# An encoder layer on one core: other distance between operands and weights, a cut product, other slots, a later preparation

## Chip, cores and metric

The kernel runs on one core of one Trainium2 chip. The metric is the device time of one execution in microseconds (us). Before the change, three runs gave 856.64, 856.88 and 858.42 us; their median is 856.88.

## What is computed

One layer of an encoder: a half-step gated FFN, a mixing part (a Fourier mixer for half of the channels, attention for the other half), a second half-step FFN and a final norm. 512 positions, 1024 channels, FFN width 2752, everything in float32. The change lies in the two FFNs alone:

```python
def swiglu(h, w_gate, w_up, w_down):
    return (jax.nn.silu(h @ w_gate) * (h @ w_up)) @ w_down

x = x + 0.5 * swiglu(rms_norm(x, ffn1_norm), ffn1_w_gate, ffn1_w_up, ffn1_w_down)
...
x = x + 0.5 * swiglu(rms_norm(x, ffn2_norm), ffn2_w_gate, ffn2_w_up, ffn2_w_down)
return rms_norm(x, final_norm)
```

## The kernel before

**High and low parts.** Each float32 operand is split into a high part, rounded to the type fp32r (a cast on ACT), and a low part (the rest, a subtraction on DVE, helper `lows`, L118). A product is three matmuls: high x high, high x low, low x high. Each matmul of a 128x128 weight tile is a pair: a weight load (PEld in the profile) and the matmul itself.

**The stages of one FFN** (`ffn`, called twice, n_ = 0 and 2). The width of 2752 is 21 blocks of 128 and a tail "t" of 64. `groups` cuts the blocks in four groups. The first group is *plain*: gate and up products of 512 columns (`gate`), then the down products of the group. All other blocks go through a seven-product scheme (Strassen's, in the form with 15 additions; `seven`, `step`, `multiply`), which computes gate and up of one block from seven products of half the size in place of eight. Its moving operands are the tile `rt` (seven combinations of the normalized input h, high and low, 256 columns), made once per FFN by `operands`; its stationary operands are sums and differences of the gate and up weights, made per block by `prepare`.

**Order.** For each later group, first a run of five or six blocks through `seven` (one block ahead of the group: blocks 4 to 9, 10 to 15, 16 to 20 in the first FFN, 3 to 8, 9 to 14, 15 to 20 in the second), then the eight down products (`down`, output blocks d = 0 to 7, 512 columns), and behind d = 0 the last product of the run's last block (`rest`, step 9). So there are six runs. In a run, block j has the steps 0 (a11), 1 (a12), 9 of the block before (a22), 3 (s1), 4 (s2), 5 (s4), 6 (s3): each is one `multiply` of twelve pairs, four 128-row pieces by three passes, 256 columns wide, at L382. Steps 0, 4, 6 and 9 accumulate in one PSUM bank (r), steps 3 and 5 in another (q), step 1 in a third (p). `kept` (L390) copies an intermediate state of a bank to SBUF on ACT: p1 after step 0, p5 after step 3, u2 after step 4. Step 6 goes on writing bank r, so it must wait for the copy u2.

**Preparation.** While block j is multiplied, `prepare` makes the weights of block j + 1. It issues two DMAs of 512 KB on SP's queue (raw_g, raw_u) and returns eight pieces of work, which are emitted between the steps as `PIECES` says: casts of high parts on ACT (L343 for pairs such as s1 and s2, L352 for a22), their low parts on DVE (L118) and the sums and differences on DVE (L358). The pieces of the first block of a run are emitted among the down products of the group before.

**Slots.** The weights' high and low parts lie in the tile `ring`: 12 slots of 4 KB per partition. The first eight are `own`, the last four `shared`; the shared ones are also the `plain` slots that the down weights use. `take` gives out the slot that has been free longest, from the own ones first, or from the shared ones first if `most` is set; `give` returns a slot when the product that reads it has been emitted. `most` is set for the preparation of the last block but one of each run.

**Addresses.** `room` puts unused bytes ahead of a tile. The ring starts at byte 16512 of each partition, `at` (the FFN's activations) at 118656, `rt` at 147392; slots, pieces and passes lie multiples of 256 bytes apart.

**Queues.** On PE and SP the instructions stand in the order in which the kernel emits them. On ACT and DVE the framework's scheduler orders them by its own simulation of the program, so that a change of slots or emission can reorder those two queues. In the mixing part between the FFNs the order of all queues is written out by hand; the change does not reach it.

Of the kernel before, what the change touches and what calls it, by code (L numbers as in the profile page):

```python
# [29 lines left out]
HALF = S // 2  # L30
USES = "a11", "a12", "s1", "s2", "s4", "s3", "a22"
PIECES = (0, 2, 2, 1, 1, 1, 1)
KH = KD // 2
HI_DVE = ("f0", "f1")
SWAP_DMA = ("q1", "q2", "q3")

# [43 lines left out]
def encoder(ctx, tc, A, out):  # L80
    nc = tc.nc
# [5 lines left out]
    def room(pool, n):  # L87


        pool.tile([P, n // 4], F32, name=f"room{len(rooms)}")  # L90
        rooms.append(n)
# [6 lines left out]
    def bank(name):  # L98
        return pp.tile([P, S], F32, tag="bank", name=name)
# [150 lines left out]
    def ffn(norm, after, wgu, wd, wdt, groups, opening, closing):  # L250
# [6 lines left out]
        with tc.tile_pool(name=f"act{n_}", bufs=1) as ap, tc.tile_pool(name=f"sums{n_}", bufs=2) as sp:  # L257
            room(ap, 192)
            at = ap.tile([P, PLACES, 2, S], F32R, name=f"at{n_}")
            room(ap, 64)  # L260
            rt = ap.tile([P, 7, 2, KH, HALF], F32R, name=f"rt{n_}")
            wt = []
            free, where = list(range(PLACES)), {}
# [5 lines left out]
            own, shared = slots[:KD], slots[KD:]  # L269
# [26 lines left out]
            def operands(rp, i0, i1):  # L296
                for i in range(i0, i1):
                    b = sp.tile([P, 4, HALF], F32, tag="raw_g", name=f"b{n_}_{i}")
                    for o, k in ((0, i), (2, i + KH)):
                        nc.vector.scalar_tensor_tensor(  # L300
# [15 lines left out]
            def back(ts):  # L316
                plain[:] = [t for t in plain if all(t is not q for q in ts)]

            def take(most):

                pool = (shared or own) if most else (own or shared)
                taken.append(pool.pop(0))
                return taken[-1]

# [2 lines left out]
                    taken[:] = [q for q in taken if q is not t]  # L327
                    (shared if any(t is q for q in slots[KD:]) else own).append(t)

            def prepare(j, most=False):  # L330

                g = sp.tile([P, KD * P], F32, tag="raw_g", name=f"raw_g{n_}_{j}")
                u = wp.tile([P, KD * P], F32, tag="raw", name=f"raw_u{n_}_{j}")
                for t, c in ((g, 2 * j), (u, 2 * j + 1)):
                    nc.sync.dma_start(out=t.rearrange("p (a b) -> p a b", b=P), in_=wgu[c])
                a11, a12, a21, a22 = g[:, :S], g[:, S:], u[:, :S], u[:, S:]
                s12 = sp.tile([P, 2 * S], F32, tag="s12", bufs=1, name=f"s12_{n_}_{j}")
                s34 = sp.tile([P, 2 * S], F32, tag="s34", bufs=1, name=f"s34_{n_}_{j}")
                w = {}

                def both(names, src):
                    hi, lo = (take(most and names[0] != "a11") for _ in range(2))
                    nc.scalar.copy(hi, src)  # L343
                    lows(lo, src, hi)
                    for i, n in enumerate(names):
                        w[n] = tuple(t[:, i * S : (i + 1) * S] for t in (hi, lo))
                    w[max(names, key=USES.index), "slots"] = hi, lo

                def single(n, src):
                    t = take(False)  # L350
                    hi, lo = t[:, :S], t[:, S:]
                    nc.scalar.copy(hi, src)  # L352
                    lows(lo, src, hi)
                    w[n] = hi, lo
                    w[n, "slots"] = (t,)

                def combine(out, a, b, op):
                    nc.vector.tensor_tensor(out=out, in0=a, in1=b, op=op)  # L358

                return w, [  # L360
                    (both, ("a11", "a12"), g),
                    (combine, s12[:, :S], a21, a22, ALU.add),
                    (combine, s12[:, S:], s12[:, :S], a11, ALU.subtract),
                    (both, ("s1", "s2"), s12),
                    (single, "a22", a22),
                    (combine, s34[:, :S], a11, a21, ALU.subtract),
                    (combine, s34[:, S:], a12, s12[:, S:], ALU.subtract),
                    (both, ("s3", "s4"), s34),
                ]

            def seven(js, done):

                done = [done]
                banks = {}

                def multiply(ps, wn, on, w, first):

                    (whi, wlo), (mhi, mlo) = w[wn], (part[on][:, i] for i in range(2))
                    for i in range(KH):
                        ks = slice(i * P, (i + 1) * P)  # L380
                        for o, (a, b) in enumerate(((whi, mhi), (whi, mlo), (wlo, mhi))):
                            nc.tensor.matmul(  # L382
                                ps, a[:, ks], b[:, i], start=first and i == 0 and o == 0,
                                stop=i == KH - 1 and o == 2, skip_group_check=not first,
                            )
                    give(*w.get((wn, "slots"), ()))

                def kept(ps, n, j):
                    t = sp.tile([P, HALF], F32, tag=n, name=f"{n}{n_}_{j}")
                    nc.scalar.copy(t, ps)  # L390
                    return t

                def step(j, w, n):
                    b = banks.setdefault(j, {})
                    if n == 0:
                        b["r"] = bank(f"r{n_}_{j}")[:, :HALF]
                        multiply(b["r"], "a11", "b11", w, True)
                        b["p1"] = kept(b["r"], "p1", j)
                    elif n == 1:
                        ps = bank(f"p2{n_}_{j}")[:, :HALF]  # L400
                        multiply(ps, "a12", "b21", w, True)
                        b["g"] = tp.tile([P, S], F32, tag="g", name=f"g{n_}_{j}")
                        nc.vector.tensor_tensor(out=b["g"][:, HALF:], in0=ps, in1=b["p1"], op=ALU.add)
                    elif n == 3:
                        b["q"] = bank(f"q{n_}_{j}")[:, :HALF]
                        multiply(b["q"], "s1", "t1", w, True)
                        b["p5"] = kept(b["q"], "p5", j)
                    elif n == 4:
                        multiply(b["r"], "s2", "t2", w, False)
                        b["u2"] = kept(b["r"], "u2", j)  # L410
                    elif n == 5:
                        multiply(b["q"], "s4", "b22", w, False)
                        nc.vector.tensor_tensor(out=b["g"][:, :HALF], in0=b["q"], in1=b["u2"], op=ALU.add)
                        nc.scalar.activation(b["g"], b["g"], AF.Silu)
                    elif n == 6:
                        multiply(b["r"], "s3", "t3", w, False)
                        b["u"] = tp.tile([P, S], F32, tag="u", name=f"u{n_}_{j}")
                        nc.scalar.copy(b["u"][:, :HALF], b["r"])
                        nc.vector.tensor_tensor(
                            out=b["u"][:, :HALF], in0=b["u"][:, :HALF], in1=b["p5"], op=ALU.add  # L420
                        )
                    elif n == 9:
                        multiply(b["r"], "a22", "t4", w, False)
                        u, i = b["u"], place(j)
                        h, l = at[:, i, 0], at[:, i, 1]
                        nc.scalar.copy(u[:, HALF:], b["r"])  # L426
                        nc.vector.tensor_tensor(out=u, in0=b["g"], in1=u, op=ALU.mult)  # L427
                        nc.scalar.copy(h, u)
                        lows(l, u, h)
                        del banks[j]  # L430

                for s in range(7 * len(js)):
                    i, n = divmod(s, 7)
                    if n == 2 and i:
                        step(js[i - 1], done[i - 1][0], 9)
                    if n == 0 and i + 1 < len(js):
                        done.append(prepare(js[i + 1], i + 1 == len(js) - 2))
                        ahead = list(done[-1][1])
                    if n != 2:
                        step(js[i], done[i][0], n)  # L440
                    if i + 1 < len(js):
                        for _ in range(PIECES[n]):
                            f, *a = ahead.pop(0)
                            f(*a)
                return lambda: step(js[-1], done[-1][0], 9)
# [27 lines left out]
            for gi, group in enumerate(groups):  # L473
                last = gi == len(groups) - 1
# [3 lines left out]
                else:  # L478
# [8 lines left out]
                    for i, c in enumerate(left):  # L487
                        pss.setdefault(c // 2, []).append(gate(c, by_dma=i in (1,) if n_ else i > 0))
                        if due:
                            j = due.pop(0)  # L490
# [3 lines left out]
                        while len(parts) * len(left) > (len(left) - 1 - i) * KH:  # L494
                            o = parts.pop(0)
# [14 lines left out]
                for d in range(KD):  # L510
# [5 lines left out]
                    ps = bank(f"dn{n_}_{d}_{gi}")  # L516
# [3 lines left out]
                    for _ in range(len(group) - (last and d < 2)):  # L520
                        next(steps)
                    waiting.append((d, ps, steps))
                    if d == 1 and not last:
                        ready = prepare(groups[gi + 1][0] + 1)
                        ahead.extend(ready[1])
                    if d == 0:
# [904 lines left out]
```

## Time and profile before

| | |
|---|---|
| median of three runs | 856.88 us |
| span of the profiled execution | 855.1 us |
| matmuls, and weight loads | 5434 each |
| matmuls at L382 | 2940 (1680 into r, 840 into q, 420 into p) |
| bytes moved by DMA | 89.25 MB, on average 104 GB/s |

The profiled execution's own device time is not listed beside its span; the median of the runs is 1.8 us above the span. The page gives busy time for each engine, the chain of work that ended last, and groups of like instructions: line, engine, operation, output<-inputs, shapes, count | busy us, mean ns of one | idle time before. Matmuls are pipelined and their ends are modelled, so a matmul's duration is longer than the period at which they follow each other. Stretches (from:to in us) give width, busy time and, in brackets, the instructions in them; where no engine is chosen, in the order PE, PEld, DVE, ACT, POOL; then granted clock, share of DMA and GB/s. Rows of the chain in order of time give start, length, engine, tile, line and count.

### The profile page before, as it was taken

What the parts mean: (1) busy time and instruction counts of PE and PEld (TensorE: products, weight loads), DVE (VectorE), ACT (ScalarE), POOL (GpSimd) and SP (SyncE); (2) the same over time, 40 slices, a digit from 0 to 9 for tenths busy, and PEclk for the clock granted to TensorE, in tenths of its full rate; (3) what the DMA queues carried; (4) which work ended last, traced back from release to release, by engine and by line L of the source; (5) the groups of instructions that cost most, each with busy time, mean ns of one, the idle gap of its engine ahead of it and who ended that gap; (6) DMA issues with size and microseconds to landing.
All of it is one profiled execution on the core that took longest, in us unless ns stands there. A gap on an engine that the chain in (4) does not pass through costs nothing.

```text
span 855.1 us, 13706 instructions
## 1 busy us (share of the span) xinstructions
PE 846.4 (99%) x5434; PEld 765.5 (90%) x5434; DVE 641.5 (75%) x1007; ACT 467.9 (55%) x781; POOL 33.3 (4%) x35
## 2 busy tenths in 40 slices
PE   9999999999999999999999999999999999999996
PEld 7878998899989998889988888899989998899986
DVE  7998985488756937699999478999846985488453
ACT  7763764266524635677776347656632764266352
POOL 0110000000000000222000000100000000000001
PEclk9999999999999999999999999999999999999998
DMA  6664322323243113414020224553232331323213
GB/s 250 164 157 157 118 88 74 118 99 127 74 145 109 48 56 111 148 50 136 26 74 26 99 70 116 120 196 108 77 117 100 118 106 56 117 100 113 67 43 99
DMA packets 31424, 89.25 MB, mean 104 GB/s; under 512 B 3712, under 2 KB 9344, under 8 KB 31232
## 3 DMA queue, kind: packets, MB, share of 16 engines
q1 hardware_dynamic: 28320, 82.87, 28.6%
q0 software_dynamic: 2496, 4.99, 3.2%
q8 instruction: 42, 0.69, 0.3%
q10 hardware_dynamic: 544, 0.52, 0.2%
q14 instruction: 22, 0.18, 0.1%
HBM read 83.91 MB, written 2.10 MB: 101 GB/s over the span
## 4 chain that ended last, share of the span: by engine, by line
PE 97%; DVE 1%; DMA 0%; issue 0%; ACT 0%; POOL 0%; POOLq 0%; DVEq 0%; ACTq 0%
PE r L382 23%; PE q L382 12%; PE dn L157 8%; PE dn L155 8%; PE dn L156 8%; PE p L382 6%; PE mix L155 3%; PE mix L157 3%; PE mix L156 3%; PE gu L632 3%; PE gu L155 2%; PE gu L157 2%; PE gu L156 2%; PE mix L1122 2%; PE mix L1079 2%; PE mix L928 1%
## 5 line engine op out<-in xcount | busy, mean ns | idle before, releaser
L382 PE MATMUL r<-rt,ring 128*128 128x256 f32 x1680 | 216.8, 280 | 0.0
L382 PEld LDWEIGHTS r<-rt,ring 128*128 128x128 f32 x1680 | 205.6, 188 | 2.6
L157 PE MATMUL dn<-at,ring 128*128 128x512 f32 x300 | 117.0, 390 | 0.5 <-DVE ring L118 0.5
L155 PE MATMUL dn<-at,ring 128*128 128x512 f32 x300 | 117.0, 390 | 0.0
L156 PE MATMUL dn<-at,ring 128*128 128x512 f32 x300 | 116.7, 389 | 0.0
L382 PE MATMUL q<-rt,ring 128*128 128x256 f32 x840 | 109.8, 279 | 0.0
L382 PEld LDWEIGHTS q<-rt,ring 128*128 128x128 f32 x840 | 103.5, 188 | 0.0
L468 DVE SCALAR_TENSOR_TENSOR gx<-dn,gx 128x512 f32<-128x512 f32 x61 | 42.0, 688 | 75.2 <-PE dn L157 75.2
L118 DVE TENSOR_TENSOR ring<-s,ring 128x1024 fp32r<-128x1024 f32 x70 | 85.3, 1220 | 16.5 <-PE r L382 10.5
L147 ACT CAST ring<-raw_dn 128x768 fp32r<-128x768 f32 (+3 forms) x58 | 45.5, 787 | 87.0 <-PE dn L156 70.6
L343 ACT CAST ring<-s 128x1024 fp32r<-128x1024 f32 x70 | 73.5, 1050 | 34.8 <-PE r L382 17.9
L157 PEld LDWEIGHTS dn<-at,ring 128*128 128x128 f32 x300 | 56.3, 188 | 13.0 <-DVE ring L118 1.1
L156 PEld LDWEIGHTS dn<-at,ring 128*128 128x128 f32 x300 | 56.3, 188 | 11.3
L155 PEld LDWEIGHTS dn<-at,ring 128*128 128x128 f32 x300 | 56.3, 188 | 11.3
L118 DVE TENSOR_TENSOR ring<-raw_dn,ring 128x768 fp32r<-128x768 f32 (+3 forms) x58 | 51.6, 892 | 6.1 <-ACT ring L147 4.1
L382 PE MATMUL p<-rt,ring 128*128 128x256 f32 x420 | 54.9, 279 | 0.0
L118 DVE TENSOR_TENSOR ring<-raw_g,ring 128x1024 fp32r<-128x1024 f32 x35 | 42.8, 1223 | 14.7 <-PE p L382 8.4
L382 PEld LDWEIGHTS p<-rt,ring 128*128 128x128 f32 x420 | 51.7, 188 | 0.0
L343 ACT CAST ring<-raw_g 128x1024 fp32r<-128x1024 f32 x35 | 36.8, 1051 | 21.5 <-DMA raw_g<-in_wgu 8.8
L352 ACT CAST ring<-raw_u 128x512 fp32r<-128x512 f32 x35 | 21.8, 622 | 33.5 <-PE dn L157 15.1
L427 DVE TENSOR_TENSOR u<-g,u 128x512 f32<-128x512 f32 x35 | 24.0, 686 | 16.0 <-ACT u L426 16.0
L224 POOL TENSOR_TENSOR r<-ms,mhalf 128x4 f32<-128x4 f32 (+1 forms) x5 | 5.9, 1179 | 679.9 <-DVE ms L217 679.9
(309 smaller groups left out, 1584.4 us busy)
## 6 DMA issues: line engine op xcount, KB each, us to landing
raw_g<-in_wgu SPq DMA_DIRECT2D x35, 512.0 KB, 3.7
raw_u<-in_wgu SPq DMA_DIRECT2D x35, 512.0 KB, 4.3
raw_dn<-in_wd SPq DMA_DIRECT2D x40, 384.0 KB, 3.1
raw_gu<-in_wgu SPq DMA_DIRECT2D x12, 512.0 KB, 3.6
raw_o<-in_wo SPq DMA_DIRECT2D x8, 512.0 KB, 3.5
raw_dn<-in_wd SPq DMA_DIRECT2D x8, 448.0 KB, 3.3
raw_wq<-in_wins SPq DMA_DIRECT2D x4, 512.0 KB, 4.6
raw_f<-in_winf SPq DMA_DIRECT2D x4, 512.0 KB, 3.5
```

The source lines that it names most:

```text
L118: nc.vector.tensor_tensor(out=lo, in0=src, in1=asf(hi), op=ALU.subtract)
L147: nc.scalar.copy(hi[:, :n, :], raw[:, :n, :])
L155: nc.tensor.matmul(ps, whi, mhi, start=first, stop=False)
L156: nc.tensor.matmul(ps, whi, mlo, start=False, stop=False)
L157: nc.tensor.matmul(ps, wlo, mhi, start=False, stop=last)
L343: nc.scalar.copy(hi, src)
L352: nc.scalar.copy(hi, src)
L382: nc.tensor.matmul(ps, a[:, ks], b[:, i], start=first and i == 0 and o == 0, stop=i == KH - 1 and o == 2, skip_group_check=not first,)
L427: nc.vector.tensor_tensor(out=u, in0=b["g"], in1=u, op=ALU.mult)
L468: nc.vector.scalar_tensor_tensor(out=x[d][:, t], in0=ps[:, t], scalar=0.5, in1=x[d][:, t], op0=ALU.mult, op1=ALU.add)
L632: nc.tensor.matmul(pss[c], w[:, k % 2, c], m[k], start=k == 0 and m is hh and w is hi, stop=k == KD - 1 and w is lo,)
L1079: nc.tensor.transpose(pts[n][:, c * P : (c + 1) * P], prob[t, b, c][:, kc * P : (kc + 1) * P], ident)
```

## The change

It has four parts, in `ffn` alone.

- `room(ap, 64)` ahead of `rt` becomes `room(ap, 192)`. In the built program `rt` then starts at byte 147520 in place of 147392, and so do the tiles behind it, 128 bytes later each.
- `multiply` gets the argument `entry`, set for step 0 of the first block of a run. There the second of the twelve products (first piece, high x low) is cut in two matmuls, of columns 0 to 63 and 64 to 255.
- `take` loses its argument: the own slots are always taken first, for every block.
- In the first group of each FFN, the preparation of the first block of the first run is emitted at d = 2 in place of d = 1.

```diff
             room(ap, 192)
             at = ap.tile([P, PLACES, 2, S], F32R, name=f"at{n_}")
-            room(ap, 64)
+            room(ap, 192)
             rt = ap.tile([P, 7, 2, KH, HALF], F32R, name=f"rt{n_}")
...
-            def take(most):
+            def take():
 
-                pool = (shared or own) if most else (own or shared)
+                pool = own or shared
                 taken.append(pool.pop(0))
                 return taken[-1]
...
-                    hi, lo = (take(most and names[0] != "a11") for _ in range(2))
+                    hi, lo = (take() for _ in range(2))
...
+                def cols(i, o, entry):
+
+                    cuts = (0, HEAD, HALF) if entry and (i, o) == (0, 1) else (0, HALF)
+                    return [slice(*c) for c in zip(cuts, cuts[1:])]
+
-                def multiply(ps, wn, on, w, first):
+                def multiply(ps, wn, on, w, first, entry=False):
...
-                            nc.tensor.matmul(
-                                ps, a[:, ks], b[:, i], start=first and i == 0 and o == 0,
-                                stop=i == KH - 1 and o == 2, skip_group_check=not first,
-                            )
+                            for c in cols(i, o, entry):
+                                nc.tensor.matmul(
+                                    ps[:, c], a[:, ks], b[:, i, c], start=first and i == 0 and o == 0,
+                                    stop=i == KH - 1 and o == 2, skip_group_check=not first or entry,
+                                )
...
-                        multiply(b["r"], "a11", "b11", w, True)
+                        multiply(b["r"], "a11", "b11", w, True, j == js[0])
...
-                        done.append(prepare(js[i + 1], i + 1 == len(js) - 2))
+                        done.append(prepare(js[i + 1]))
...
-                    if d == 1 and not last:
+                    if d == (1 if gi else 2) and not last:
                         ready = prepare(groups[gi + 1][0] + 1)
```

`HEAD` is 64.

More of the change, by code (lines that the diff above doesn't have):

```diff
@@ L33 @@
 KH = KD // 2
+HEAD = 64
 HI_DVE = ("f0", "f1")
@@ L328, in give, with prepare @@
                     (shared if any(t is q for q in slots[KD:]) else own).append(t)
-            def prepare(j, most=False):
+            def prepare(j):
                 g = sp.tile([P, KD * P], F32, tag="raw_g", name=f"raw_g{n_}_{j}")
@@ L349, in single @@
                 def single(n, src):
-                    t = take(False)
+                    t = take()
                     hi, lo = t[:, :S], t[:, S:]
```

## The prediction

> **What bounds the kernel now.** I read the page first: busy time, granted clock, the chain that ended last, the costliest groups.
>
> ```profile
> span 855.1 us, 13706 instructions
> ...
> PE 846.4 (99%) x5434; PEld 765.5 (90%) x5434; DVE 641.5 (75%) x1007; ACT 467.9 (55%) x781; POOL 33.3 (4%) x35
> ...
> PE 97%; DVE 1%; DMA 0%; issue 0%; ACT 0%; POOL 0%; POOLq 0%; DVEq 0%; ACTq 0%
> ...
> L382 PE MATMUL r<-rt,ring 128*128 128x256 f32 x1680 | 216.8, 280 | 0.0
> L382 PEld LDWEIGHTS r<-rt,ring 128*128 128x128 f32 x1680 | 205.6, 188 | 2.6
> ```
>
> TensorE is the bound: 97% of the chain, with each matmul paired with a weight load of its own (5434 of each). So the time can only move through the period at which pairs start, through the number of pairs, and through waits. The mean of 280 ns is no period, since matmuls overlap; periods come from counts in stretches. The change is aimed at the pairs of line 382. They stand in six runs, so I cut the trace into those:
>
> ```profile
> 76.36:134.79 58.43, 58.43 (x492) 1.00 0.29 100
> 168.92:227.30 58.38, 58.38 (x492) 1.00 0.29 100
> 261.44:309.93 48.49, 48.49 (x408) 1.00 0.28 91
> 562.00:619.00 57.00, 57.00 (x492) 1.00 0.31 107
> 653.11:711.50 58.39, 58.39 (x492) 1.00 0.29 100
> 745.63:804.02 58.39, 58.39 (x492) 1.00 0.27 94
> sum 339.08, PE 339.08; mean PE 56.51
> ```
>
> The first number after the count is the granted clock, 1.00. The runs hold 5 x 492 + 408 = 2868 pairs in 339.08 us. One run of 492 is 1.4 us shorter than its equals, with the same program and addresses. The chain in order of time says why:
>
> ```profile
> 562.16 1.42 PE r L382 x12
> ...
> 579.31 2.91 PE r L382 x24
> 589.03 2.93 PE r L382 x24
> 598.75 2.72 PE r L382 x24
> ...
> 772.94 2.97 PE r L382 x24
> 782.98 2.83 PE r L382 x24
> ```
>
> A pair has two steady periods: 2.83 / 24 = 117.9 ns, where every run begins (562.16: 1.42 for 12) and nearly all stay, and 2.72 / 24 = 113.3 ns, which the fourth run falls into after the wait near 579 and keeps to its end, through another wait near 589. A third period belongs to the pairs of 256 columns at the end that read "at" (the timeline, and a stretch with their count):
>
> ```profile
> 829.31 0.28 PE L155 MATMUL last<-at,ring 128*128 128x256 f32 x1
> ```
> ```profile
> 829.00:837.00 8.00, 7.69 (x65) 7.88 (x66) 0.85 (x2) 1.00 0.01 2
> ```
>
> From 829.31 to 837.00 65 begin: 7.69 / 64 = 120 ns. In the built program the weights' ring starts 128 bytes past a multiple of 256, "at" too, and rt 192 past one. So 0 bytes off goes with 120 ns, 64 bytes off with 117.9 or 113.3, and the mode, once entered, persists.
>
> The slow stretches with a wait (2.97) cost 0.14 us over those without, the fast one (2.93 against 2.72) 0.21. The timeline of one wait:
>
> ```profile
> 92.11 1.57 PE L382 MATMUL q<-rt,ring 128*128 128x256 f32 x12
> ...
> 92.19 1.05 ACT L343 CAST ring<-s 128x1024 fp32r<-128x1024 f32 x1
> ...
> 93.14 0.36 ACT L390 COPY u<-r 128x256 f32<-128x256 f32 x1
> 93.56 0.89 PEld L382 LDWEIGHTS r<-rt,ring 128*128 128x128 f32 x7
> ```
>
> The cast into a slot that step 4 has just freed stands ahead of the copy of u2 in ACT's queue; the twelve matmuls of step 5 take 1.41 us, cast and copy end at 93.50, and step 6, which writes the bank that the copy reads, waits. There are 18 such waits, three in each run: in those blocks s3's high part is given a slot freed at step 4.
>
> **The change part by part.** *rt moves by 128 bytes*, so that it lies 192 bytes off the weights, modulo 256. No matmul in the trace reads at that distance. Its period is bounded by the nearest rows: 113.3 from below, 120 from above; over 2868 pairs 325.0 to 344.2 us.
>
> *The second product of each run is cut in 64 and 192 columns*: one pair more in each of six runs. No such pair is in the trace. Its bounds are 0 (if 64 columns hide in the neighbouring loads) and the mean load of 188 ns; I take a whole fast period, because a pair comes no closer than that in these stretches: 6 x 0.113 = 0.7 us (0 to 1.1). More important is what it does to the mode. All six runs now enter at 117.9, each behind the same 512-column products, so entry is repeatable; the only change of mode came behind an irregular gap between loads (the stretch at 579.31). The cut puts one short matmul under a full weight load, so it makes just such a gap at the entry. Whether 64 columns at 192 bytes lead to 113.3 the trace cannot say. I take 113.3: it is the state that survived a wait, while in the slow one 17 of 18 waits left things as they were and one led out; in the whole trace no wait leads from fast to slow. 2868 x 0.11333 = 325.0 us.
>
> The Trainium skill, "TensorE: Matmul & The Clock Gate", Part 2 (step by step), speaks against this: TensorE has two independent SBUF read ports, and loading the next weights takes no read bandwidth from the running matmul. By that rule 128 bytes of address change nothing, and this part is worth 0 in place of the gain above. Two periods at one address do not refute it, but the rows at 0 and 64 bytes, 120 against 113.3 to 117.9 ns, do not fit it.
>
> *Plain slots taken last.* Before, the preparation of a run's last block but one took plain slots first; following the first-in-first-out lists by hand, s3's high part then waits on step 4 in three blocks of a run. After, it takes slots freed at step 4 in every prepared block: 5 + 5 + 4 + 5 + 5 + 5 = 29 waits, and in the built program's ACT queue the cast stands ahead of the copy of u2 in all of them (before, in the first three, with another cast of the same length in one case). At 113.3 ns a wait costs 0.21: 29 x 0.21 = 6.1 us. Bounds: 18 x 0.14 = 2.5, if ACT gets by as now, and 0.3 each, 8.7, if two pieces queue up.
>
> The first down weights come free a block earlier in return, and with them one low part of 0.89 us on DVE moves into blocks that also prepare. DVE is what hides the preparations:
>
> ```profile
> 579.46:598.59 19.13, 19.13 (x168) 19.00 (x168) 18.16 (x27) 13.27 (x23) 0.00 (x0) 1.00 0.34 115
> ```
> ```profile
> L118 DVE TENSOR_TENSOR ring<-raw_dn,ring 128x768 fp32r<-128x768 f32 (+3 forms) x58 | 51.6, 892 | 6.1 <-ACT ring L147 4.1
> ```
>
> Two fast blocks hold 18.16 us of DVE work, 9.1 a block. A fast block with one wait lasts 84 x 0.1133 + 0.21 = 9.7. Another 0.89 makes 10.0, so up to 0.3 a run could come out as a wait for a low part: 0 to 1.8 us; I take 0.7.
>
> *First preparation a block later.* It applies to the first group of each FFN only. SP now issues raw_dn 2 ahead of the two raw tiles of 512 KB, and ACT's cast and DVE's low part of dn 2 move ahead of the preparation's. Now that low part is late:
>
> ```profile
> 60.62 0.39 PE L155 MATMUL dn<-at,ring 128*128 128x512 f32 x1
> 60.85 0.39 PE L156 MATMUL dn<-at,ring 128*128 128x512 f32 x1
> 61.12 0.55 DVE L118 TENSOR_TENSOR ring<-raw_dn,ring 128x384 fp32r<-128x384 f32 x1
> ...
> 61.72 0.50 PE L157 MATMUL dn<-at,ring 128*128 128x512 f32 x1 [0.48 <-DVE ring L118]
> ...
> 67.13 1.22 DVE L118 TENSOR_TENSOR ring<-s,ring 128x1024 fp32r<-128x1024 f32 x1
> ```
>
> A product starts 0.23 us after the one before (60.62 to 60.85), but 0.87 passes between 60.85 and 61.72: 0.64 us that should go. Bounds 0 and 0.8 (with the refill behind it). The preparation ends later by one output block, 11 x 0.23 = 2.5 us; its last low part now ends at 68.35, and the run that reads it begins at 76.36, so 8.0 us of down products cover it; without that cover it would cost those 2.5. Nothing else is queued behind these DMAs before dn 3.
>
> **Sum.** The six runs: 325.0 + 6.1 + 0.7 + 0.7 = 332.5 against 339.1, so -6.6; the first preparation -0.6; together -7.2. The profiled span was 855.1; the runs' median is 856.88, 1.8 more, which I keep as what lies around the span. 855.1 - 7.2 + 1.8 = 849.7 us. Its own range is 846 (waits stay at 18) to 853 (DVE and ACT at their upper bounds).
>
> **The rivals.** *The slow mode stays* (the address and the cut are inert): 2868 x 0.1179 = 338.1, 29 waits at 0.14 = 4.1, cut 0.7: 342.9, +3.8; -0.6: 860.1 us. For it: every run enters slow, and the added waits are certain by the queue. Against it: the fourth run shows that the other period can be had. It decides as soon as fewer than some 30% of the pairs run at 113.3, since each tenth of them is worth 1.3 us. This is the inert outcome that the Trainium skill's rule names; the change then does not do what its first two parts could.
>
> *192 bytes off is a bad distance, as 0 is*: 2868 x 0.120 = 344.2; step 5 then lasts 1.44 us, so a wait shrinks to about 0.12, 29 x 0.12 = 3.5; cut 0.7: 348.4, +9.3, -0.6: 865.6 us. For it: 120 is the one other period seen; against it: 0 and 192 are different distances, and 64 already avoided it.
>
> *Half*: the cut leads into the fast mode, but with five waits a run it is lost again about midway: mean of the forecast and the slow case, 854.9. For it: modes change at waits. Against it: the wait at 589 did not change it.
>
> *Fast, without added waits*: 325.0 + 18 x 0.21 + 0.7 = 329.5, -9.6, -0.6: 846.7; with no wait at all 842.9. Against it: the queue's order.
>
> **How the numbers follow.** Forecast 0.46, slow mode stays 0.22, half 0.13, bad distance 0.13, fast without added waits 0.06. A change of 0.2% is 1.7 us, about what a measurement tells from none. Faster: 0.46 + 0.06 + 0.10 of half = 0.62; same: 0.03 of half and 0.05 of slow (860.1 is +0.4%, less one or two waits) = 0.08; slower: 0.17 + 0.13 = 0.30. The range runs from 844 to 861: it leaves out the bad distance and the extreme of no waits.
>
> **What would show it.** Chain pieces of twelve pairs at 1.36 from the first or second step of each of the six runs show the mode; 1.41 or 1.42 there shows the slow rival, 1.44 the bad distance. Five stretches of 24 a run near 2.93, with ACT's copy of u2 as releaser, show the waits; three would show my slot count wrong. The product at 61.72 without idle time shows the first preparation. A 64-column matmul followed by a gap over 0.19 us would make the cut dearer. The prediction falls if fewer than half the pairs run at 113.3, or if DVE's low parts end more waits than ACT.

## The result, and the profile after

The changed kernel takes 866.07 us (median of four runs, 864.66 to 866.57). The kernel before took 856.82 beside it (856.64 to 858.42). The ratio is 1.0096, with a 95% interval of 1.0079 to 1.0112: slower by 1%, where 849.7 us, 0.8% faster, had been forecast. The profiled execution took 866.55 us, of which the span is 864.7.

The page of the changed kernel: span, busy time, the chain by engine, and four groups, three of which now have idle time ahead of them (the last two columns: idle us, and what ended most of it).

```profile
span 864.7 us, 13711 instructions
...
PE 846.8 (98%) x5440; PEld 760.3 (88%) x5440; DVE 643.1 (74%) x1007; ACT 468.9 (54%) x781; POOL 32.4 (4%) x35
...
PE 92%; ACT 4%; DVE 1%; issue 1%; DMA 1%; POOL 0%; POOLq 0%; DVEq 0%; ACTq 0%
...
L389 PE MATMUL r<-rt,ring 128*128 128x256 f32 x1686 | 215.4, 280 | 4.5 <-ACT u L397 4.2
...
L156 PE MATMUL dn<-at,ring 128*128 128x512 f32 x300 | 117.2, 391 | 3.3 <-ACT ring L148 3.3
L158 PE MATMUL dn<-at,ring 128*128 128x512 f32 x300 | 117.4, 391 | 1.9 <-DVE ring L119 1.9
L157 PE MATMUL dn<-at,ring 128*128 128x512 f32 x300 | 116.8, 389 | 0.0
```

The first and the third pass of the down products (L155 and L157 there) in the page of the kernel before:

```profile
L157 PE MATMUL dn<-at,ring 128*128 128x512 f32 x300 | 117.0, 390 | 0.5 <-DVE ring L118 0.5
L155 PE MATMUL dn<-at,ring 128*128 128x512 f32 x300 | 117.0, 390 | 0.0
```

TensorE had 97% of the chain before and has 92% now. Six matmuls more are the six cuts. The rest of the loss is waiting: ahead of step 6 (bank r, for ACT's copy of u2), and ahead of the first and third pass of a down product. Where they stand, in the stretches of the six runs (width, TensorE's busy time, its matmuls, then the granted clock):

```profile
76.30:135.39 59.09, 57.80 (x494) 1.00 0.30 99
170.45:229.33 58.88, 58.05 (x494) 1.00 0.29 98
265.07:313.83 48.76, 48.18 (x410) 1.00 0.28 88
565.83:623.45 57.62, 57.62 (x494) 1.00 0.33 110
659.18:717.75 58.57, 57.65 (x495) 1.00 0.30 98
753.45:811.87 58.42, 57.54 (x495) 1.00 0.26 86
sum 341.34, PE 336.83; mean PE 56.14
```

The runs grew by 341.34 - 339.08 = 2.3 us, and everything outside them by the other 7.3 of the 9.6. Neither number shows what happened inside. For that I counted all pairs of the scheme (the six runs, and the last product of each behind the first down product) by the distance from one start to the next, without those at a wait or a cut. Before, 345 had up to 115 ns and 2559 more; now 2034 have up to 115 and 830 more. That is worth (2559 - 830) x 4.6 ns = 8.0 us, a gain. But there are 33 waits in place of 18, and the time that the pairs at them take beyond 113.3 ns each is 12.1 us in place of 3.0. With 0.8 for the cuts the three make +1.9; 2.3 were measured.

One wait, in the timeline of ACT's and TensorE's instructions (start, length, operation; idle time before and its releaser in brackets):

```profile
111.14 0.84 ACT L148 CAST ring<-raw_dn 128x768 fp32r<-128x768 f32 x1 [0.33 <-PE r L389]
...
111.88 0.62 ACT L435 CAST at<-u 128x512 fp32r<-128x512 f32 x1
112.40 1.04 ACT L344 CAST ring<-s 128x1024 fp32r<-128x1024 f32 x1
...
113.35 0.36 ACT L397 COPY u<-r 128x256 f32<-128x256 f32 x1
...
113.76 0.62 PE L389 MATMUL r<-rt,ring 128*128 128x256 f32 x3 [0.54 <-ACT u L397]
```

Three casts, 2.5 us together, stand ahead of a copy that has to be done within the 1.36 us of step 5. The forecast saw the third of them. The first is that of the first down weights. By the lists of slots, the plain slot that it fills held the low part of s1 and s2, which step 4 reads last: the cast may start when the copy may, and stands ahead of it. (The kernel before casts these weights at 124.98.) The brackets say 0.54, but the start before 113.76 lies 0.82 us back: matmuls have modelled ends, so the idle column shows a wait only where it outlasts the matmul's drawn end.

Not every wait is like this one. Of the 33, six have the cast of a down weight ahead of the copy, each time into a plain slot that the low part of s1 and s2 held until step 4: 0.8 to 1.0 us each, 5.3 in all. In five, 0.3 to 0.6 us each and 2.2 in all, no down weight is there, but the cast of `at` comes so late that it pushes the cast of s3 and s4 back. The other 22 take 4.6 us, 0.21 on average, as forecast. One of the five, in the same view of ACT:

```profile
185.69 0.62 ACT L435 CAST at<-u 128x512 fp32r<-128x512 f32 x1 [0.71 <-DVE u L434]
186.22 1.05 ACT L344 CAST ring<-s 128x1024 fp32r<-128x1024 f32 x1
187.17 0.36 ACT L397 COPY u<-r 128x256 f32<-128x256 f32 x1
```

Between the runs, in the same timeline of the changed kernel (ACT, DVE, then TensorE):

```profile
234.95 0.83 ACT L148 CAST ring<-raw_dn 128x768 fp32r<-128x768 f32 x1 [0.64 <-PE r L389]
...
235.81 0.96 DVE L119 TENSOR_TENSOR ring<-raw_dn,ring 128x768 fp32r<-128x768 f32 x1 [0.52 <-ACT ring L148]
...
235.83 0.50 PE L156 MATMUL dn<-at,ring 128*128 128x512 f32 x1 [0.80 <-ACT ring L148]
236.17 0.40 PE L157 MATMUL dn<-at,ring 128*128 128x512 f32 x1
236.83 0.50 PE L158 MATMUL dn<-at,ring 128*128 128x512 f32 x1 [0.26 <-DVE ring L119]
237.17 0.39 PE L156 MATMUL dn<-at,ring 128*128 128x512 f32 x1
```

The cast of the second down weights waited for "PE r L389": the last pairs of step 9 of the run's last block, which stand behind the first down product. By the lists that block now holds two of the four plain slots (the low part of s1 and s2, until step 4, and a22, until step 9). So the second down product waits for the cast, its third pass for the low part, and each wait has a longer gap behind it (0.34 in place of 0.23). There are four such places, and a fifth behind the first run, where only the third pass waits: there the high part goes into the slot free since step 4, the low part into that of a22. By starts, a place costs 1.0 to 1.9 us; together they cost 7.6 us, 0.3 more than the 7.3 outside the runs, where the idle time at 61.72 is gone and other small differences stand against that.

### The profile page after: what moved, and what is told of

Read it like the earlier page. It is cut to its first block, busy times and chain, and to the rows that moved or that the text cites. A ratio compares the mean times of both kernels' runs of the same rounds, so it can differ in the third digit from the quotient of the medians.

```text
span 864.7 us, 13711 instructions
## 1 busy us (share of the span) xinstructions
PE 846.8 (98%) x5440; PEld 760.3 (88%) x5440; DVE 643.1 (74%) x1007; ACT 468.9 (54%) x781; POOL 32.4 (4%) x35
## 4 chain that ended last, share of the span: by engine, by line
PE 92%; ACT 4%; DVE 1%; issue 1%; DMA 1%; POOL 0%; POOLq 0%; DVEq 0%; ACTq 0%
PE r L389 20%; PE q L389 9%; PE dn L158 8%; PE dn L157 8%; PE dn L156 8%; PE p L389 5%; PE mix L156 3%; PE mix L158 3%; PE mix L157 3%; PE gu L639 3%; PE gu L156 3%; PE gu L158 3%; PE gu L157 3%; ACT ring L344 2%; PE mix L1129 2%; PE mix L1086 2%
## 5 line engine op out<-in xcount | busy, mean ns | idle before, releaser
L389 PE MATMUL r<-rt,ring 128*128 128x256 f32 x1686 | 215.4, 280 | 4.5 <-ACT u L397 4.2
L389 PEld LDWEIGHTS r<-rt,ring 128*128 128x128 f32 x1686 | 202.8, 188 | 10.5 <-ACT u L397 7.2
L157 PE MATMUL dn<-at,ring 128*128 128x512 f32 x300 | 116.8, 389 | 0.0
L389 PE MATMUL q<-rt,ring 128*128 128x256 f32 x840 | 107.4, 277 | 0.0
L389 PEld LDWEIGHTS q<-rt,ring 128*128 128x128 f32 x840 | 101.2, 188 | 0.0
L157 PEld LDWEIGHTS dn<-at,ring 128*128 128x128 f32 x300 | 56.3, 188 | 11.3
L389 PE MATMUL p<-rt,ring 128*128 128x256 f32 x420 | 53.7, 277 | 0.0
L389 PEld LDWEIGHTS p<-rt,ring 128*128 128x128 f32 x420 | 50.6, 188 | 0.0
L435 ACT CAST at<-u 128x512 fp32r<-128x512 f32 x35 | 21.7, 621 | 14.9 <-DVE u L434 14.9
```

What stands on the lines that cost most here:

```text
L157: nc.tensor.matmul(ps, whi, mlo, start=False, stop=False)
L389: nc.tensor.matmul(ps[:, c], a[:, ks], b[:, i, c], start=first and i == 0 and o == 0, stop=i == KH - 1 and o == 2, skip_group_check=not fi ...
```

## The experiments

The column "six runs" is the sum of the kernel's stretches as above. The last column counts all pairs of the scheme, as above, by their distance from start to start. (467 of the 471 of off0 stand at 115 ns itself, among others of 117 to 122.)

| kernel | median us | before, same chip | ratio, 95% interval | six runs us | pairs up to / over 115 ns |
|---|---|---|---|---|---|
| slots_back | 849.53 | 856.17 | 0.9918 (0.9888 to 0.9948) | 334.52 | 1934 / 963 |
| slots_only | 871.15 | 856.17 | 1.0174 (1.0147 to 1.0202) | 344.62 | 575 / 2295 |
| offset_only | 851.17 | 856.17 | 0.9939 (0.9919 to 0.9960) | 332.69 | 2120 / 784 |
| cut_only | 856.57 | 856.17 | 1.0007 (0.9990 to 1.0025) | 339.83 | 435 / 2463 |
| u2_first | 842.98 | 856.63 | 0.9847 (0.9831 to 0.9862) | 326.87 | 2664 / 268 |
| after_u2 | 854.68 | 856.63 | 0.9975 (0.9966 to 0.9985) | 330.52 | 2642 / 278 |
| off0 | 861.32 | 856.63 | 1.0059 (1.0046 to 1.0072) | 343.30 | 471 / 2433 |
| off128 | 864.53 | 856.63 | 1.0096 (1.0081 to 1.0110) | 346.23 | 15 / 2889 |
| u2_all | 842.82 | 857.82 | 0.9826 (0.9812 to 0.9839) | 325.87 | 2844 / 90 |
| u2_no_cut | 854.46 | 857.82 | 0.9960 (0.9948 to 0.9973) | 337.81 | 0 / 2940 |
| u2_off64 | 855.35 | 857.82 | 0.9969 (0.9958 to 0.9981) | 338.42 | 7 / 2927 |
| u2_early | 844.12 | 857.82 | 0.9839 (0.9825 to 0.9852) | 325.86 | 2844 / 90 |

### One part undone, and three parts alone

slots_back is the changed kernel with the slots of before; the other three are parts put into the kernel before.

```diff
# slots_back, against the changed kernel
-            def take():
+            def take(most):
-                pool = own or shared
+                pool = (shared or own) if most else (own or shared)
...
-                        done.append(prepare(js[i + 1]))
+                        done.append(prepare(js[i + 1], i + 1 == len(js) - 2))
# slots_only, against the kernel before: these lines the other way round
# offset_only, against the kernel before
-            room(ap, 64)
+            room(ap, 192)
             rt = ap.tile([P, 7, 2, KH, HALF], F32R, name=f"rt{n_}")
# cut_only, against the kernel before
-                        multiply(b["r"], "a11", "b11", w, True)
+                        multiply(b["r"], "a11", "b11", w, True, j == js[0])
```

> The changed kernel with the old rule for the slots (shared ones first for a run's last block but one); address, cut and later preparation stay. Theory S (the slots cost the time: the last block of a run holds two plain slots, so the second down weights wait for one, and high casts that wait on step 4 hold up ACT): no wait over 0.3 us at the head of the down products, 18 waits of 0.2 in the runs, pairs mostly at 113.3 ns: 845 to 850 us, faster than before. Rival P (pairs at 113.3 outrun ACT and DVE, whatever the slots): waits of 0.5 to 0.9 us in the runs and at the down products stay, 858 to 866 us.

> The kernel before with the new rule for the slots alone. Theory S: waits of 1.0 to 1.9 us at the head of four or five groups of down products (some 7 us) and five longer waits a run, with pairs near 117.9 ns: 866 to 877 us, slower than the changed kernel or equal to it. Rival P: pairs stay slow enough for ACT and DVE, so at most the 11 added waits of 0.14 us: 857 to 860 us.

> The kernel before with rt 192 bytes off the weights, nothing else. If the address decides the period (A): every run enters at 113.3 ns, 846 to 849 us. If the cut is what leads into 113.3 (C): runs enter at 117.9, change only at waits, 851 to 857 us.

> The kernel before with the second product of each run cut in 64 and 192 columns, rt at 64 bytes as before. If the cut alone leads into 113.3 (C): runs enter at 113.3, 846 to 850 us. If it needs the address (A, or both together): runs enter at 117.9, 857 to 858.5 us.

The old slots take the changed kernel from 866.07 to 849.53; the new slots alone take the kernel before from 856.17 to 871.15. So this one part costs 15 to 17 us, and the other three gain 0.8%. The waits view of slots_only (engine and tile, what it waited for: us, times, longest) has the same three rows as the changed kernel, at the addresses of before:

```profile
PE r L382 <- ACT u L390: 3.4, 6, 0.6
PE dn L155 <- ACT ring L147: 3.3, 4, 0.9
PE dn L157 <- DVE ring L118: 2.4, 6, 0.7
```

In slots_back the two rows of dn are gone. Its 18 waits in the runs did not come out at 0.2 each, as expected: they take 4.7 us, the longest over 0.6, again behind a late cast of `at`. So waits of that kind come with the old slots too. The distance alone gains 0.6%, though all six runs of offset_only enter at 118 ns: each leaves that period behind one of its waits. The cut alone, at 64 bytes, leads no run into 113 ns and changes nothing that can be told.

### The copy ahead of the cast

The three casts say that the wait is a matter of ACT's order. One edge puts the cast of s3 and s4 behind the copy of u2, once with the old slots and once with the new ones.

```diff
# u2_first against slots_back, and after_u2 against the changed kernel
-                    nc.scalar.copy(t, ps)
+                    copies[n] = nc.scalar.copy(t, ps).ins
...
                             f, *a = ahead.pop(0)
-                            f(*a)
+                            with tc.issue_after(copies["u2"]) if n == 6 else nullcontext():
+                                f(*a)
```

> slots_back with one more edge: on ACT's queue the cast of s3 and s4 is issued behind the copy of u2. Slots are those of before, nothing else changes. In slots_back 18 waits of 0.15 to 0.68 us in front of step 6 add up to 4.7 us, and 963 of 2897 pairs ran at 117.9 ns, 4.4 us over 113.3. Theory Q (the waits are the copy of u2 standing behind a cast of 1.05 us in ACT's queue, and the slow period returns only through a wait): both go, 849.5 - 4.7 - 4.4 + 0.3 for the six pieces behind the down products = 840.7 us; a wait is left in block 18 at most. Half theory (waits go, period still changes on its own): 844.8. Rival R (the cast is late next, or its low part on DVE, and the product of s4 or s3 of the next block waits for it): the waits move, 848 to 851.

> The changed kernel with that same edge on ACT's queue and its own slots. It splits the cost of the slots rule in its two suspected places. In the changed kernel the waits for the copy of u2 add up to 12.1 us in 31 places, and the waits at the second and third down product behind four runs and the first to 7.7. Theory Q: the first kind goes but for the last blocks of runs, where a cast of s1 and s2 still stands ahead, about 2.5 us; the second kind stays whole: 866.1 - 12.1 + 2.5 = 856.5 us, 854 to 859, and the down products still wait 1.0 to 1.6 us each group. Rival (both kinds have one cause, slots that come free too late, and the queue's order only shows it): the time stays above 862.

u2_first took 842.98 us, between theory Q (840.7) and its half (844.8). The trace decides for Q: with the waits the second period went as well. The sum of Q had taken the waits of an execution of 851.45 us off the median of 849.53; taken off 851.45 it gives 842.7. The single wait that was left, in block 18, did lead 181 pairs back to 118 ns. after_u2 took 854.68. Its waits view:

```profile
PE dn L158 <- ACT ring L150: 3.3, 4, 0.9
PE r L391 <- ACT u L399: 2.3, 4, 0.6
PE dn L160 <- DVE ring L121: 1.9, 5, 0.7
```

The two rows of the down products are to the digit those of the changed kernel (3.3 and 1.9): that part of the cost is one of slots, not of queue order. In the runs five waits are left, 3.8 us in all, of 33 with 12.1; 2.5 had been expected. So the difference between the changed kernel and slots_back (16.5 us on medians, 15.0 between the profiled spans) has two causes, 12.1 - 4.7 = 7.4 us of waits in the runs and 7.6 at the down products. Ahead of step 6 it is the order of ACT's queue, which the new slots made worse; at the down products it is a slot held until step 9.

### The distance

In the kernel before `room(ap, 64)` ahead of `rt` becomes 128 (off0) or 256 (off128). The two names, and the expectations that go with them, have the distances the wrong way round. `rt` started at byte 147392, the ring at 16512. With 64 bytes more `rt` starts at 147456, 130944 = 511 x 256 + 128 bytes behind the ring; with 192 more it starts at 147584, 131072 = 512 x 256 bytes behind it. So off0 lies 128 bytes off the weights, modulo 256, and off128 lies 0 bytes off.

> The kernel before with rt 0 bytes off the weights modulo 256, nothing else. Theory A (the distance modulo 256 sets the period; at 0 it is the 120 ns of the pairs that read at): all pairs near 120 ns, 2868 x 0.120 = 344.2 against 339.1, less 18 waits that shrink by 0.02 each: 861 us, ratio 1.006. Rival (the address is inert, the period is chance of the entry): 856, pairs at 117.9 or 113.3.

> The kernel before with rt 128 bytes off the weights modulo 256. Theory A with a period that falls with the distance: pairs at 113.3 for more than half of the runs, 850 to 853 us, as with 192. Theory A with the banks in pairs of 128 (128 stands as 0 does): 120 ns, 861. Rival (the address is inert): 856, mostly 117.9.

Read by what was built, 0 bytes (off128) came out at 864.53 us and 128 bytes (off0) at 861.32. For 0 bytes 861 had been expected; that the kernel named off0 took just that is chance. The period is the one that theory A gave for 0 bytes, 120 ns. Its sum was short because it set 344.2, which holds no waits, against 339.1, which does: with 18 waits of 0.12 it comes to 346.4, and 346.23 were measured. For 128 bytes the form of theory A that sets 128 beside 0 gave 861, and came out. The inert address, 856, is refuted by both. The chain in order of time (start, length, pieces of 12 or 24 pairs), off128 (0 bytes) and then off0 (128 bytes):

```profile
79.98 1.44 PE q L382 x12
81.42 1.44 PE r L382 x12
...
84.30 3.03 PE r L382 x24
```
```profile
80.96 1.44 PE r L382 x12
...
86.84 1.42 PE p L382 x12
```

At 0 bytes 12 pairs take 1.44 us, 120 ns a pair, almost throughout, and none of the 18 waits changes it. At 128 bytes all six runs enter at 120 ns, and behind the first wait most pieces last 1.42 or 1.43 (118.9 ns on average over all pairs without a wait). The stretches grew from 339.1 to 346.2 us at 0 bytes and to 343.3 at 128. Only `rt` and the tiles behind it moved, and the ring did not: whether the distance counts or `rt`'s own address modulo 256, no run shows.

### No wait left

u2_all puts the edge on every cast of a preparation; the other three take one thing out of it.

```diff
# u2_all, against u2_first
-                            with tc.issue_after(copies["u2"]) if n == 6 else nullcontext():
+                            with tc.issue_after(copies["u2"]) if copies.get("u2") else nullcontext():
# u2_no_cut, against u2_all
-                    cuts = (0, HEAD, HALF) if entry and (i, o) == (0, 1) else (0, HALF)
+                    cuts = (0, HALF)
# u2_off64, against u2_all
-            room(ap, 192)
+            room(ap, 64)
             rt = ap.tile([P, 7, 2, KH, HALF], F32R, name=f"rt{n_}")
# u2_early, against u2_all
-                    if d == (1 if gi else 2) and not last:
+                    if d == 1 and not last:
```

> u2_first with the edge on all casts of a preparation, so that the last cast ahead of a copy of u2 (raw_g of block 20, in block 18) goes behind it too. u2_first had one wait left, 0.21 us and its refill, and behind it 181 pairs at 117.9 ns. Theory M (the period changes at waits alone, and the cut sets it at the entry): no wait is left, no pair changes: 843.0 - 181 x 0.0046 - 0.2 = 841.9 us. Rival: 843 or more, since the casts behind the copy come too late for block 20.

> u2_all without the cut of the second product. Theory M: without the cut all six runs enter at 117.9 ns, as in offset_only, and with no wait left nothing leads out: 841.9 + 2868 x 0.0046 - 6 x 0.1 = 854.4 us, almost all pairs at 117.9. Rival (192 bytes lead to 113.3 by themselves, after some pairs): 841 to 844.

> u2_all with rt at its old distance of 64 bytes, with the cut. Theory M with what cut_only showed (at 64 bytes the cut does not lead to 113.3): pairs at 117.9 throughout, 855 us. Rival (the cut is enough once no wait disturbs): 842.

> u2_all with the first preparation at d = 1, as before the change. If the later preparation is worth what the prediction gave it, the product at 62 us waits again for its low part, 0.6 to 0.8 us, and the time is 842.5 to 842.8 us, 0.6 to 0.9 above u2_all, in the trace more surely than in the medians. Rival (the later preparation only moves the wait): same time.

u2_all beats both kernels: 842.82 us, ratio 0.9826 to the kernel before. (841.9 had been expected. On medians it does not stand apart from u2_first, 842.98 on another chip; the spans are 840.8 and 842.4. The trace shows what theory M says: no wait in the runs, and no pair that changes.) Its stretches, first and last with the sum, and its chain:

```profile
75.51:131.41 55.90, 55.90 (x495) 1.00 0.31 105
...
733.72:789.62 55.90, 55.90 (x494) 1.00 0.31 98
sum 325.87, PE 325.87; mean PE 54.31
```
```profile
85.33 1.36 PE p L391 x12
86.69 1.36 PE r L391 x12
...
92.13 2.72 PE r L391 x24
```

All five long runs last 55.9 us, and step 5 with step 6 takes 2.72 where the changed kernel had 2.93 to 3.03. Of its 90 pairs over 115 ns 18 stand at the six entries; the other 72 are the last products behind the first down products, which begin without a cut and run at 118. Without the cut, or at 64 bytes with it, nothing is left of that. The chain of u2_no_cut:

```profile
81.32 1.41 PE q L391 x12
82.73 2.83 PE r L391 x24
85.56 1.41 PE p L391 x12
```

All 2940 pairs of it run at 118 ns, from the first to the last, and u2_off64 does the same. Against u2_all they take 11.6 and 12.5 us more. So distance and cut are worth some 12 us together, and neither alone brings a run to 113 ns, once no wait disturbs (no run leaves out both): the cut leads into 113 ns only at 192 bytes, and at 192 bytes a run that enters at 118 keeps it. That offset_only gained all the same was the work of its waits.

In u2_early the wait at the down product of 62 us is back, here in its timeline of TensorE:

```profile
61.29 0.39 PE L159 MATMUL dn<-at,ring 128*128 128x512 f32 x1
62.43 0.50 PE L160 MATMUL dn<-at,ring 128*128 128x512 f32 x1 [0.75 <-DVE ring L121]
62.77 0.40 PE L468 MATMUL dn<-at,wt 128*128 128x512 f32 x1
```

From start to start 1.14 and 0.34 us in place of 0.23 twice: 1.0 us, above the 0.6 to 0.8 expected. The medians stand 1.3 apart (842.82 and 844.12), the spans 1.4.

## Why the prediction was wrong

**The bound and the period at the entry: right, in part by luck.** TensorE's pair period decides. The changed kernel enters all six runs at 113.3 ns, as taken, and u2_no_cut shows that the cut is what leads there. But the forecast said itself that its trace could not decide between the periods; what about the cut does it, no run shows. That the state persists was right only between waits. It was argued from one run that kept it through one wait; of the 18 waits only that one fell in the fast state, so the slow state had 17, of which 16 changed nothing. In the changed kernel eleven of the 33 waits change the period, seven to 118 ns and four back to 113, and 762 pairs of the six runs had over 115: 3.5 us that the sum did not hold. It is the mechanism of the rival "half", in a smaller size.

**The step that failed: plain slots taken last.** The sum gave it "29 x 0.21 = 6.1 us", with 8.7 as the upper bound, and 0.7 for DVE. The count was nearly right (33; the four more stand in last blocks of runs), the price was not. 0.21 came from a wait with one cast ahead of the copy, and 22 waits cost that. The same paragraph said that the first down weights come free a block earlier, and followed only their low part, on DVE. That holds in the first run (cast at 111.14 in place of 124.98), but not in all: in the second their cast comes in the last block, at 225.18, where the kernel before has it at 211.84, a block ahead of the last. The step missed the cast itself. It takes 0.84 us on ACT and goes ahead of the same copy, since its slot now comes free behind step 4; five times with the first down weights and once with the second this makes waits of 0.8 to 1.0 us, 4.0 us over their price. Five waits behind a late cast of `at` are 1.2 over theirs, and the four more make 0.8. The sum is 12.1 us, 6.0 over the term, where 8.7 was the bound. u2_first and after_u2 show that the queue's order is the cause: with the copy ahead of the cast of s3 and s4 one of the 18 waits of slots_back is left, and five of the 33 of the changed kernel.

**What the step left out: who gives plain slots back.** Plain slots that the last block but one does not take are taken by the last block, which keeps one until step 9, behind the first down product. The prediction followed the first down weights alone; the second ones come late. This is the 7.6 us at the down products, which stay in after_u2 and go with the old slots. Together: 6.0 + 7.6 + 3.5 - 0.7 (no low part ended a wait inside the runs) = 16.4 us over the forecast; 866.07 - 849.7 = 16.4 were measured, so closely by chance, since terms of some 0.1 are left out.

**The cut: right.** A run of 493 pairs takes 55.90 in u2_all, and 492 x 2.72 / 24 = 55.76: 0.14 a run, 0.8 in six, where 0.7 was given.

**First preparation: right.** -0.6 was given, with 0.8 as the bound. By starts the place cost 0.75 us in the kernel before (0.87 and 0.34 in place of 0.23 twice) and costs 1.0 in u2_early. The later preparation made no run wait.

**The rule of the Trainium skill.** By the Trainium skill, "TensorE: Matmul & The Clock Gate", Part 2 (step by step), loading weights takes no bandwidth from the running matmul; from this the prediction worked out that the address would be inert. off0 and off128 move `rt` alone, with the tiles behind it, and cost 0.6% and 1.0%: for the time of these pairs the rule does not hold as the prediction read it. What in the memory or the engine does this, no run shows.

**The outcome with no wait at all** was worked out as 842.9 among the rivals; u2_all took 842.82. The parts' gain was there, and it took another order on ACT to keep it.

## What to carry to other kernels

When buffers are handed out in another order, follow each of them to its last reader, and ask for every later taker, on every queue, what it now stands ahead of: here the casts of down weights came to wait for the same step as a small copy, went ahead of it, and TensorE waited for the copy. A small copy on which TensorE's next step depends belongs ahead of casts that have time; one edge of issue order was worth some 6 us with the old slots and 10 to 11 with the new ones. Measure waits from start to start, since an idle column built on modelled ends hides the first part of each.

## What the hardware showed

- The period of pairs of 256 columns depends on where the moving operand lies. By its distance from the weights, modulo 256 bytes, it is 119.9 ns on average at 0 (off128), 118.9 at 128 (off0), and 117.8 or 113.3 at 64 and 192, at a granted clock of 1.00 in all of them. The weights stayed at one address, so its own address would sort the runs in the same way.
- At 192 bytes both periods are stable: 492 pairs without a wait stay in the one in which they begin (55.90 us and 57.95 us for the same work in u2_all and u2_no_cut). One product cut in 64 and 192 columns at the entry decides it, in six runs of six; at 64 bytes the same cut led to 113 ns in none (cut_only, u2_off64).
- At 64 and 192 bytes a wait can move the pairs from either period to the other; which wait does was not settled.
